# Two triangular inverses in step: interleaving the head pairs of an RWKV-7 scan on one Trainium2 core

## The chip, the cores and the metric

The kernel runs on one core of a Trainium2 chip. The metric is the device time of one execution in microseconds. Five engines matter: TensorE (matrix products, shown as PE, its weight loads as PEld), VectorE (DVE), ScalarE (ACT), GpSimd (POOL) and SyncE (SP), which issues most transfers.

## The reference

One inference step of a hybrid decoder layer over 576 tokens: a prompt of 512 and eight sequences of 8 sampled tokens. RWKV-7 time mixing and differential attention run as parallel branches on the same normalised input; their results are merged by gates, and a squared-ReLU MLP follows.

```python
xn = rmsnorm(x, lp['g_mix'], NORM_EPS)
P = xn @ lp['w_in']                                   # 1024 -> 5376 columns
o_a, S = rwkv7_branch(Pr, S0, lp)                     # 8 heads of 64
att = attend(q, k, v, lam)                            # 4 heads, two maps each
m = gate_a * (o_a @ lp['w_br_a']) + gate_b * (o_b @ lp['w_br_b'])
x = x + m @ lp['w_out']
x = x + jnp.square(jax.nn.relu(hn @ lp['w_up'])) @ lp['w_down']
```

What the change touches is the scan of the RWKV branch. As the reference has it, one token at a time:

```python
def step(S, inp):
    r_t, w_t, k_t, v_t, a_t, b_t = inp
    sa = jnp.einsum('bhij,bhj->bhi', S, a_t)
    S = S * w_t[:, :, None, :] + sa[..., None] * b_t[:, :, None, :] + v_t[..., None] * k_t[:, :, None, :]
    return S, jnp.einsum('bhij,bhj->bhi', S, r_t)
```

## The kernel before

**Chunks and pairs.** The kernel runs the scan in chunks of 64 tokens: eight of the prompt and one that holds the 64 sampled tokens. Within a chunk the recurrence becomes a unit triangular 64x64 system, whose inverse is computed once for each chunk and head; then a chain walks over the chunks. The eight heads are taken as four pairs, hp 0 to 3, two heads on the 128 partitions; pairs 0 and 1 form one group, 2 and 3 the other, and a group has one chain.

**Stages of a pair.** `rwkv(hp)` is a generator (L720 to L952). Its parts, which the text calls stages by letters, end at a `yield`:

- A: decay, normalised keys and the masked product matrices ABR (tiles pn, pw, pa, pk, pbn, pA; long on VectorE);
- B: transposed values and keys, and the sampled sequences' initial states (pV, pK, pI);
- C: the inverse (below);
- D: final states of the sampled sequences (pF);
- E: group norm, with a power on GpSimd and a multiplication of y by var on VectorE;
- F: output, with transposes pTy and the gate product pg.

**The inverse (L852 to L900).** X and its transpose Y hold the inverses of the diagonal blocks of size 1, 2, 4, 8, 16 and at the end 32. Four levels double the size. A level masks the matrix into DM (VectorE), makes W from DM and X by 32x32 products in the bank pW, copies W out (ScalarE), makes pZ from Y and W, adds it to X (VectorE), and transposes X into Y (VectorE). Each of these two visits of TensorE has 72 products of 32x32 by 32x32 (64 in the last two levels). Then Wc and pC, 32 products each, join 32 to 64, and TT takes the result. Every step needs the one before, so TensorE is given dense work between the visits.

**Dense work.** All large matrix products (`stream`, L154) are generators that issue one product at each step: 128x128 weights against 288 columns (296 for some of the projections). They run in split precision, three products for each block of weights; the weights come by SP's queue, ScalarE and VectorE split them into a high and a low half, and each half span of 24 products has one of two PSUM banks (pool psd). The list `waiting` holds such generators in order: the projections z of pairs 1 to 3 (144 products a pair), eight gates of branch B, five of branch A (48 each), later the output of branch B and three more gates. `take(n)` issues the next n products of that list.

**Order.** The framework orders each engine's instructions at build time by a model of durations: among those ready, the one first in program order goes. `issue_after` holds the instructions of its block back until the named one on the same engine has been issued. In the inverse `blocks` takes nine dense products so, behind each of the eight visits. Where the program stands at each moment is written by hand at the end (L1027 to L1055): `run(...)` advances the named pairs by a stage each, `take` stands between.

**Banks.** The inverses use the bank of `tbank`. `cbank(1)`, another pool's, is used by the attention before and by the output pY of the chain (L972) after.

Of the kernel before, what the change touches and what calls it, by code (L numbers as in the profile page):

```python
# [41 lines left out]
def tile_hybrid_step(ctx, tc, xT, xsT, ktab, vtab, s0T, ptab, w_in, vecs, w2a2, g2, lamv,  # L42
# [6 lines left out]
    def pool(name, bufs=1, stack=ctx, **kw):  # L49
        return stack.enter_context(tc.tile_pool(name=name, bufs=bufs, **kw))  # L50
# [4 lines left out]
    ring = {"job": 0}  # L55

    def act(out, in_, func=AF.Copy, **kw):
        ring["act"] = AE.activation(out=out, in_=in_, func=func, **kw)  # L58

    def tt(out, a, b, op, eng=None):  # L60
        ins = (eng or VE).tensor_tensor(out=out, in0=a, in1=b, op=op)  # L61
        if eng is None:
            ring["tt"] = ins
# [7 lines left out]
    def mm(out, lhsT, rhs, start=True, stop=True):  # L71
        ring["mm"] = PE.matmul(out=out, lhsT=lhsT, rhs=rhs, start=start, stop=stop)  # L72
        return ring["mm"]
# [17 lines left out]
    MUL, ADD, SUB, MAX = ALU.mult, ALU.add, ALU.subtract, ALU.max  # L91
# [12 lines left out]
    def tbank(name):  # L104
        return psc.tile([P, 512], F32, tag="t", name=name)

    def cbank(i, name):
        return (psy if i else psc).tile([P, 512], F32, tag=f"c{i}", name=name)
# [107 lines left out]
    def take(n):  # L216

        while waiting and n:
            if next(waiting[0], None) is None:
                waiting.pop(0)  # L220
            else:
                n -= 1
# [41 lines left out]
    gs = pool("gs", 2, stack=ph1)  # L264

    with tc.tile_pool(name="xin", bufs=2, reuse_waits="tile") as xin:
# [6 lines left out]
        for k in range(0, KT, 4):  # L273
            for j in range(3):
                with prio(FEED + 1000 + 10 * k + j):
                    name = f"raw_{'qkv'[j]}0_{k}"
# [142 lines left out]
    def shifted(i):  # L419
        z = zw.tile([P, 1 + NX], F32, tag="z", name=f"Z{i}")  # L420
        GE.memset(z[:, 0:1], 0.0)

        def f(ps, t0, n):
            tt(z[:, 1 + t0:1 + t0 + n], ps, R1[:, t0:t0 + n], MUL)
        yield from stream(w_in[i], KT, xh, xl, HALFX, f, f"z{i}")
        tz = zw.tile([P, 1 + NX], F32, tag="tz", name=f"tz{i}", bufs=1)
        act(tz, z, scale=v(V_MU + i))
        p = zp.tile([P, NT], F32, tag=f"P{i}" if i >= 12 else f"Pt{i // 4}", name=f"P{i}", bufs=1 if i >= 12 else 2)
        m1 = mu1[:, i:i + 1]
        stt(p[:, :NPR], z[:, 1:1 + NPR], m1, tz[:, 0:NPR], MUL, ADD)  # L430
        s3 = lambda a, o: a[:, o:o + NS].rearrange("p (b t) -> p b t", b=NB)
        stt(s3(p, NPR)[:, :, 1:], s3(z, 1 + NPR)[:, :, 1:], m1, s3(tz, 1 + NPR)[:, :, :7], MUL, ADD)
        stt(p[:, NPR::8], z[:, 1 + NPR:1 + NT:8], m1, tz[:, 1 + NT:], MUL, ADD)
        Pt[i] = p

    def zs(hp):
        return [shifted(i) for i in (hp, 4 + hp, 8 + hp)]

    def gate(g):

        gg = gs.tile([P, NT], F32, tag="gg", name=f"gg{g}")

        def ev(ps, t0, n):
            tt(gg[:, t0:t0 + n], ps, R1[:, t0:t0 + n], MUL)
            act(gg[:, t0:t0 + n], gg[:, t0:t0 + n], AF.Tanh, scale=0.5)
        yield from stream(w_in[26 + g], KT, xh, xl, HALF, ev, f"g{g}")
        nc.sync.dma_start(out=gt_d[g], in_=gg)
# [20 lines left out]
    def branch_b(d):  # L468

        if not ob:  # L470
            ob.extend(ob_halves())
        gg = rt.tile([P, NT], F32, tag="T", name=f"gb{d}", bufs=6)
        nc.sync.dma_start(out=gg, in_=gt_d[KT + d])

        def ev(ps, t0, n):
            stt(gg[:, t0:t0 + n], gg[:, t0:t0 + n], 1.0, ps, ADD, MUL)
        yield from stream(w_brb[d], HB, ob[0], ob[1], HALF, ev, f"brb_{d}")
        nc.sync.dma_start(out=gt_d[KT + d], in_=gg)
# [221 lines left out]
    def m3(ap_, n):  # L700
        q, w = ap_.shape
        return ap_.rearrange("p (o w) -> p o w", o=1).broadcast_to([q, n, w])
# [17 lines left out]
    def rwkv(hp):  # L720
        e = hp % 2
# [131 lines left out]
        for g in range(4):  # L853
            gs = slice(32 * g, 32 * g + 32)
            act(DT[gs], ABR[gs, :, 0, 32 * (g % 2):32 * (g % 2) + 32])
        Y = rt.tile([P, NCH, 32], F32, tag="Y", name=f"Y{hp}", bufs=2)
        X = rt.tile([P, NCH, 32], F32, tag="X", name=f"X{hp}", bufs=2)
# [1 line left out]
        tt(Y, Y, m3(c[:, C_I32:C_I32 + 32], NCH), ADD)  # L859
        VE.transpose(out=X, in_=Y)  # L860

        def blocks(ps, lhs, rhs, n):
            for ci in range(n):
                for g in range(4):
                    gs = slice(32 * g, 32 * g + 32)
                    last = mm(ps[gs, ci * 32:ci * 32 + 32], lhs[gs, ci], rhs[gs, ci])
            with tc.issue_after(last.ins):
                take(9)
            return ps[:, :n * 32].rearrange("p (c s) -> p c s", c=n)

        with tc.issue_after(ring["mm"].ins):
            take(1)
        for l in range(1, 5):

            n = NCH if l < 3 else 8
            DM = rt.tile([P, NCH, 32], F32, tag="DM", name=f"DM{hp}_{l}")
            tt(DM[:, :n], DT[:, :n], m3(c[:, C_LM + 32 * l:C_LM + 32 * l + 32], n), MUL)
            W = rt.tile([P, NCH, 32], F32, tag="W", name=f"W{hp}_{l}")
            act(W[:, :n], blocks(tbank(f"pW{hp}{l}"), DM, X, n))
            tt(X[:, :n], X[:, :n], blocks(tbank(f"pZ{hp}{l}"), Y, W, n), ADD)  # L880
            VE.transpose(out=Y[:, :n], in_=X[:, :n])
        TT = rb_.tile([P, NCH, 64], F32, tag="TT", name=f"TT{hp}")
        pW = tbank(f"pWc{hp}")
        W = rt.tile([P, NCH, 32], F32, tag="W", name=f"Wc{hp}")
        quads = [(slice(64 * par, 64 * par + 32), slice(64 * par + 32, 64 * par + 64)) for par in range(2)]
        for ci in range(8):
# [1 line left out]
                mm(pW[b1, ci * 32:ci * 32 + 32], ABR[b0, ci, 0, 32:64], X[b0, ci])  # L888
        for b0, b1 in quads:
            act(W[b1, :8], pW[b1, :256].rearrange("p (c s) -> p c s", c=8))  # L890
        pC = tbank(f"pC{hp}")
        for ci in range(8):
            for b0, b1 in quads:
                mm(pC[b0, ci * 32:ci * 32 + 32], W[b1, ci], Y[b1, ci])
        for b0, b1 in quads:
            act(TT[b0, :8, 32:64], pC[b0, :256].rearrange("p (c s) -> p c s", c=8))
            act(TT[b0, :, 0:32], Y[b0])
            act(TT[b1, :, 32:64], Y[b1])
            GE.memset(TT[b0, 8:, 32:64], 0.0)
            GE.memset(TT[b1, :, 0:32], 0.0)  # L900

        own[e] = ST, KBt, TT, ABR, pc
        yield
# [113 lines left out]


    gens = [rwkv(hp) for hp in range(4)]

    def run(*stages):
        for hp in stages:
            while Pt[8 + hp] is None:
                take(2)
            next(gens[hp], None)

    waiting += zs(1) + zs(2) + zs(3) + [gate(g) for g in range(KT, 2 * KT)]  # L1027
    ga = [gate(g) for g in range(KT)]
    waiting += ga[:5]
    run(0, 0)  # L1030
    take(221)
    run(0, 1, 1)
    take(106)
    run(1)
    chain(0)
    run(2, 0, 1, 2, 3)
    take(291)
    run(2, 0, 1, 3)
    take(38)
    run(3)  # L1040
    waiting += [x for d in range(KT) for x in [branch_b(d)] + ga[5:][d:d + 1]]
    run(0, 1)
    chain(1)
# [237 lines left out]
    for t0, n in LAST:  # L1281
        span, last = slice(t0, t0 + n), []
# [172 lines left out]
```

## Time and profile before

| | us |
|---|---|
| three timed runs | 1013.26, 1016.58, 1019.81 |
| median | 1016.58 |
| the profiled execution | 1013.8 |
| its span | 1012.0 |
| mean granted TensorE clock | 0.989 of full speed |

The span runs from the first to the last instruction that the profile shows; 1.8 us lie around it. "Busy" of TensorE is the time in which at least one product was in its pipeline, so that it isn't the same as TensorE at its peak. A row of the order in time has the start, the duration from the first start to the last end, the engine, the line (often a helper's, such as L72, the one of all products, or L58 and L61), the operation, output and inputs by the program's names, the shape, and the count. In brackets stands the idle time ahead of it on its engine, with what ended it. A row of a table by stretches has, after the stretch and its length, the busy time of PE, PEld, DVE, ACT and POOL (of one engine where a single engine or tile is asked for), each with its count, then the granted clock, the share of the transfer engines and GB/s. The stretch of the four inverses and two chains runs from about 227 to 492 us.

### The profile page before, as it was taken

How to read it: one execution, taken by the hardware profiler on the slowest of the kernel's cores; microseconds unless marked ns; L12 is line 12 of the kernel's file. 1: busy time of each engine (PE TensorE's matmuls, PEld its weight loads, DVE VectorE, ACT ScalarE, POOL GpSimd, SP SyncE). 2: the span in 40 equal slices, each digit the busy share in tenths (PEclk: the TensorE clock that was granted, in tenths of full speed). 3: DMA queues.
4: the chain of work that ended last, by engine and by line, in shares of the span. 5: the costliest groups of instructions: out<-in, count | busy, mean ns of one | idle time of the engine just before them, and what ended most of it. 6: DMA issues, size and time to landing. Idle time of an engine off the chain costs nothing. (4 is left out here: it accounts for less than half of the span.)

```text
span 1012.0 us, 24407 instructions
## 1 busy us (share of the span) xinstructions
PE 976.8 (97%) x10012; PEld 918.6 (91%) x10012; DVE 694.5 (69%) x1445; ACT 495.7 (49%) x1086; POOL 101.0 (10%) x179
## 2 busy tenths in 40 slices
PE   8999989999999998999989999999999999999996
PEld 8999978898888888878789999999999999999996
DVE  6698665864965788344579888966666666666744
ACT  6576554353544353453244666644444444444732
POOL 2511102301010431000210111000000000000001
PEclk9999999999999999999999999999999999999998
DMA  7412564121111135312367632222222222221402
GB/s 264 150 66 86 181 204 135 44 66 52 53 45 58 58 111 160 99 68 92 114 207 220 198 121 99 76 102 85 94 84 87 92 85 84 85 84 43 134 3 94
DMA packets 50834, 105.75 MB, mean 104 GB/s; under 512 B 6067, under 2 KB 8115, under 8 KB 50595
## 3 DMA queue, kind: packets, MB, share of 16 engines
q1 hardware_dynamic: 47442, 96.95, 29.9%
q0 software_dynamic: 1648, 5.35, 1.4%
q10 hardware_dynamic: 1632, 1.89, 0.5%
q8 instruction: 79, 1.29, 0.5%
q14 instruction: 33, 0.26, 0.1%
HBM read 89.38 MB, written 14.78 MB: 103 GB/s over the span
## 5 line engine op out<-in xcount | busy, mean ns | idle before, releaser
L72 PE MATMUL ps_dn<-q,hi_dn 128*128 128x288 f32 x768 | 154.8, 296 | 0.0
L72 PEld LDWEIGHTS ps_dn<-q,hi_dn 128*128 128x128 f32 x768 | 122.9, 188 | 1.4
L72 PE MATMUL ps_dn<-q,lo_dn 128*128 128x288 f32 x384 | 113.3, 295 | 0.0
L72 PE MATMUL ps_g<-xh,hi_g 128*128 128x288 f32 x256 | 80.2, 313 | 0.0
L72 PE MATMUL ps_g<-xh,lo_g 128*128 128x288 f32 x256 | 79.0, 308 | 0.0
L72 PE MATMUL ps_g<-xl,hi_g 128*128 128x288 f32 x256 | 78.9, 308 | 0.0
L72 PEld LDWEIGHTS ps_dn<-q,lo_dn 128*128 128x128 f32 x384 | 72.1, 188 | 0.0
L72 PE MATMUL ps_z<-xh,hi_z 128*128 128x296 f32 (+1 forms) x224 | 67.8, 303 | 1.3 <-DVE Z L61 0.7
L72 PE MATMUL ps_z<-xh,lo_z 128*128 128x288 f32 (+1 forms) x224 | 68.6, 306 | 0.0
L72 PE MATMUL ps_z<-xl,hi_z 128*128 128x288 f32 (+1 forms) x224 | 67.9, 303 | 0.0
L61 DVE TENSOR_TENSOR ya<-ya,ps_dn 128x288 f32<-128x288 f32 x96 | 43.3, 451 | 29.4 <-PE ps_dn L72 29.4
L58 ACT ACTIVATE hi_dn<-raw_dn 128x512 fp32r<-128x512 f32 x48 | 30.1, 628 | 56.1 <-PE ps_dn L72 56.1
L1191 PE MATMUL ua<-h_b,hi 128*128 128x288 f32 x256 | 53.3, 299 | 0.9 <-ACT p L58 0.9
L1191 PE MATMUL ux<-h_t,hi 128*128 128x288 f32 x256 | 52.3, 296 | 0.0
L58 ACT ACTIVATE c<-c 128x288 f32<-128x288 f32 x112 | 48.5, 439 | 6.5 <-DVE c L61 4.9
L72 PEld LDWEIGHTS ps_g<-xl,hi_g 128*128 128x128 f32 x256 | 48.7, 190 | 2.5 <-issue 0.8
L72 PEld LDWEIGHTS ps_g<-xh,hi_g 128*128 128x128 f32 x256 | 48.7, 190 | 2.5 <-issue 0.8
L72 PEld LDWEIGHTS ps_g<-xh,lo_g 128*128 128x128 f32 x256 | 48.6, 190 | 1.4
L58 ACT ACTIVATE hi<-a 128x1024 fp32r<-128x1024 f32 (+1 forms) x32 | 27.0, 845 | 43.0 <-PE ps_dn L72 34.8
L61 DVE TENSOR_TENSOR lo<-s,hi 128x1024 fp32r<-128x1024 f32 x32 | 39.2, 1224 | 10.5 <-ACT hi L58 10.4
L72 PE MATMUL ps_dn<-q,w 128*128 128x320 f32 (+1 forms) x336 | 46.3, 298 | 0.0
L72 PEld LDWEIGHTS ps_dn<-q,w 128*128 128x128 f32 x336 | 45.2, 190 | 0.1
(399 smaller groups left out, 2816.0 us busy)
## 6 DMA issues: line engine op xcount, KB each, us to landing
a<-in_w_up_dram SPq DMA_DIRECT2D x32, 512.0 KB, 3.3
raw_dn<-in_w_down_dram SPq DMA_DIRECT2D x64, 256.0 KB, 2.8
raw_g<-in_w_in_dram SPq DMA_DIRECT2D x32, 256.0 KB, 3.1
raw_z<-in_w_in_dram SPq DMA_DIRECT2D x28, 256.0 KB, 2.9
gt_d<-gg SPq DMA_DIRECT2D x16, 288.0 KB, 2.4
g<-gt_d SPq DMA_DIRECT2D x16, 288.0 KB, 3.4
kp<-in_ktab_dram SPq DMA_DIRECT2D x16, 256.0 KB, 4.7
vp<-in_vtab_dram SPq DMA_DIRECT2D x16, 256.0 KB, 4.2
```

The costliest lines, as they stand in the source:

```text
L58: ring["act"] = AE.activation(out=out, in_=in_, func=func, **kw)
L61: ins = (eng or VE).tensor_tensor(out=out, in0=a, in1=b, op=op)
L72: ring["mm"] = PE.matmul(out=out, lhsT=lhsT, rhs=rhs, start=start, stop=stop)
L1191: ring["mm"] = PE.matmul(out=ps[:, :288], lhsT=l[:, k], rhs=hb[blk][:, h, k], start=start and i == 0, stop=i == 11, skip_group_check=skip)
```

## The change

The inverse yields behind each visit instead of taking dense products itself. `invert(0, 1)` and `invert(2, 3)` step two pairs in turn, and take six dense products behind each double visit. The second pair of a group has the chain's output bank instead of the shared one. So that both are ready, pair 1's stages A and B come ahead of pair 0's inverse, and stage E of pairs 0 and 1 and stage B of pair 3 come ahead of the joint inverse of 2 and 3. The free takes change with it: 106 becomes 150, 291 becomes 340; those of an inverse were 73 for one pair and are 61 for two. What isn't taken there stays in the list for later.

```diff
-        def blocks(ps, lhs, rhs, n):
+        def blocks(name, lhs, rhs, n):
+            ps = cbank(1, name) if e else tbank(name)
             for ci in range(n):
                 for g in range(4):
                     gs = slice(32 * g, 32 * g + 32)
-                    last = mm(ps[gs, ci * 32:ci * 32 + 32], lhs[gs, ci], rhs[gs, ci])
-            with tc.issue_after(last.ins):
-                take(9)
+                    mm(ps[gs, ci * 32:ci * 32 + 32], lhs[gs, ci], rhs[gs, ci])
             return ps[:, :n * 32].rearrange("p (c s) -> p c s", c=n)
 
-        with tc.issue_after(ring["mm"].ins):
-            take(1)
         for l in range(1, 5):
...
-            act(W[:, :n], blocks(tbank(f"pW{hp}{l}"), DM, X, n))
-            tt(X[:, :n], X[:, :n], blocks(tbank(f"pZ{hp}{l}"), Y, W, n), ADD)
+            act(W[:, :n], blocks(f"pW{hp}{l}", DM, X, n))
+            yield True
+            tt(X[:, :n], X[:, :n], blocks(f"pZ{hp}{l}", Y, W, n), ADD)
             VE.transpose(out=Y[:, :n], in_=X[:, :n])
+            yield True
...
-        pW = tbank(f"pWc{hp}")
+        pW = cbank(1, f"pWc{hp}") if e else tbank(f"pWc{hp}")
...
+        yield True
-        pC = tbank(f"pC{hp}")
+        pC = cbank(1, f"pC{hp}") if e else tbank(f"pC{hp}")
...
+    def invert(*hps):
+
+        with tc.issue_after(ring["mm"].ins):
+            take(1)
+        more = True
+        while more:
+            for hp in hps:
+                more = next(gens[hp], None)
+            with tc.issue_after(ring["mm"].ins):
+                take(6)
+
     waiting += zs(1) + zs(2) + zs(3) + [gate(g) for g in range(KT, 2 * KT)]
     ga = [gate(g) for g in range(KT)]
     waiting += ga[:5]
     run(0, 0)
     take(221)
-    run(0, 1, 1)
-    take(106)
-    run(1)
+    run(1, 1)
+    take(150)
+    invert(0, 1)
     chain(0)
     run(2, 0, 1, 2, 3)
-    take(291)
-    run(2, 0, 1, 3)
+    take(340)
+    run(0, 1, 3)
     take(38)
-    run(3)
+    invert(2, 3)
```

## The prediction

> **What bounds the kernel now.** I read the page from the top, then the share of each engine in the stretch that the change touches (220 to 500 us), then the order of TensorE's instructions there, then VectorE's at the one place where TensorE stands still.
>
> ```profile
> span 1012.0 us, 24407 instructions
> ...
> PE 976.8 (97%) x10012; PEld 918.6 (91%) x10012; DVE 694.5 (69%) x1445; ACT 495.7 (49%) x1086; POOL 101.0 (10%) x179
> ```
>
> TensorE is the bound: 35 us of the span are left idle, spread over the kernel. A gain must come from idle time or from time in which TensorE counts as busy and does little. Both can be seen in the inverses. First one visit of pair 0 (its 72 small products), in order of time; columns are start, duration, instruction, count.
>
> ```profile
> 227.07 0.29 PE L72 MATMUL ps_z<-xl,hi_z 128*128 128x288 f32 x1
> 227.29 0.82 PE L72 MATMUL pW<-X,DM 32*32 32x32 f32 x72
> 228.04 0.40 PE L72 MATMUL ps_z<-xh,lo_z 128*128 128x288 f32 x1
> 228.27 0.29 PE L72 MATMUL ps_z<-xh,hi_z 128*128 128x288 f32 x1
> 228.40 0.29 PE L72 MATMUL ps_z<-xl,hi_z 128*128 128x288 f32 x1
> ...
> 229.20 0.29 PE L72 MATMUL ps_z<-xl,hi_z 128*128 128x288 f32 x1
> 229.43 0.82 PE L72 MATMUL pZ<-W,Y 32*32 32x32 f32 x72
> ```
>
> From 228.27 to 229.20 lie seven dense products: 0.133 us each. The median small product lasts 0.19 us:
>
> ```profile
> L72 PE MATMUL pW<-X,DM x1088: 185/192/257, 227.3 to 440.0; 32*32 32x32 f32 x182
> ```
>
> so the last of the 72 starts 0.82 - 0.19 = 0.63 us after the first: 8.9 ns apart. A visit's period is 229.43 - 227.29 = 2.14 us. Nine dense products take 1.19, 72 small ones 0.64; **0.31 us are left over, the price of going from dense to small and back**. It sits at the edges: dense to small takes 0.22 instead of 0.13, and the first dense product behind the block holds the next off for 0.23.
>
> Second, pair 2's third visit, on TensorE and on VectorE.
>
> ```profile
> 397.05 0.29 PE L72 MATMUL ps_g<-xh,lo_g 128*128 128x288 f32 x1
> 400.03 1.18 PE L72 MATMUL pW<-X,DM 32*32 32x32 f32 x72 [2.69 <-DVE X L61]
> 401.15 0.61 PE L72 MATMUL ps_g<-xh,hi_g 128*128 128x288 f32 x1
> ...
> 403.56 0.82 PE L72 MATMUL pZ<-W,Y 32*32 32x32 f32 x72
> ```
>
> ```profile
> 396.05 0.74 DVE L61 TENSOR_TENSOR obh<-ob,obh 128x576 fp32r<-128x576 f32 x1
> 398.49 0.76 DVE L61 TENSOR_TENSOR y<-y,var 128x576 f32<-128x576 f32 x1 [1.69 <-POOL var L238]
> 399.16 0.45 DVE L61 TENSOR_TENSOR Y<-DT,cst_sb 128x288 f32<-128x288 f32 x1
> 399.53 0.45 DVE L61 TENSOR_TENSOR X<-X,pZ 128x288 f32<-128x288 f32 x1
> ```
>
> The group norm of pairs 0 and 1 (y times var, stage E of the program) stands in VectorE's queue ahead of pair 2's X and waits 1.69 us for GpSimd's power; the products allowed at this point are used up, and TensorE idles. Without the wait the block would have started at 397.05 + 0.22 = 397.27: 2.76 us lost. Then the granted clock (the column behind the busy times) falls:
>
> ```profile
> 398.00:400.00 2.00, 0.00 (x0) 0.00 (x0) 1.51 (x4) 0.00 (x0) 1.29 (x5) 1.00 0.37 133
> 400.00:402.00 2.00, 1.97 (x75) 1.91 (x76) 2.00 (x6) 0.85 (x2) 0.00 (x0) 0.51 0.19 67
> 402.00:404.00 2.00, 2.00 (x57) 1.77 (x59) 1.70 (x4) 0.00 (x0) 0.00 (x0) 0.64 0.69 213
> ```
>
> and that visit takes 403.56 - 400.03 = 3.53 us for 2.14: 1.39 us more. **The stall costs 4.15 us.** [...]
>
> **The change, part by part.**
>
> *Half the switches.* Before, each of 4 pairs makes 10 visits (8 of blocks, then Wc and pC), each with a switch to small and back: 40. After, the two pairs' blocks follow each other: 20 double visits. Nothing else changes in the small work, and the dense products taken out of the visits are done elsewhere at 0.133. So 20 x 0.31 = 6.2 us. The price of small to small across two pairs isn't in the trace: from below nothing, as between the small products within a block; from above the same 0.31, and the saving is nil. I take nothing: every small product has its own weights already, so the pair's edge is like any other. [...]
>
> *Stage E leaves pair 2's inverse.* It is now put after `take(340)`, ahead of the joint inverse of 2 and 3. GpSimd's power and VectorE's wait for it remain, but in a stretch where dense products are free to go: minus 4.15. What it costs if that cover fails: up to the same, in another place. Pair 1's inverse has a small wait of the same kind:
>
> ```profile
> 292.17 0.75 PE L72 MATMUL pW<-X,DM 32*32 32x32 f32 x64 [0.55 <-DVE X L61]
> ```
>
> I count it as gone: minus 0.55.
>
> *Slack in a double visit.* The added wait: the six products stand behind the second pair's block, and the dense streams are in order (two banks), so all dense work queues behind that block when its X or W is late. Own block to own next block is the partner's 0.64 + 6 x 0.133 + 0.31 = 1.75 us, against 1.19 + 0.31 = 1.5 before.
>
> ```profile
> 228.15 0.41 ACT L58 ACTIVATE W<-pW 128x288 f32<-128x288 f32 x1
> ```
>
> ```profile
> 230.29 0.46 DVE L61 TENSOR_TENSOR X<-X,pZ 128x288 f32<-128x288 f32 x1 [0.74 <-PE pZ L72]
> 230.78 0.48 DVE L881 STREAM_TRANSPOSE Y<-X 128x288 f32<-128x288 f32 x1
> ```
>
> W needs 0.45 us. For X: the block that began at 229.43 ends at 230.25, X is ready at 230.75, 0.50 later. The second pair's X stands behind the first's X and Y (0.46 + 0.48): 0.94 + 0.50, less the 0.64 by which its block ends later, 0.80 of 1.75. So about 1 us is spare; it hides one foreign VectorE instruction of the size above (0.45 to 0.76), not two. No cost.
>
> *Pair 1's preparation comes ahead.* It must be done before the joint inverse can go on. Before, from its first product to its X:
>
> ```profile
> 245.52 1.28 PE L72 MATMUL pn<-cst_sb,sq 128*128 128x2 f32 x10
> ```
>
> ```profile
> 281.35 0.47 DVE L860 STREAM_TRANSPOSE X<-Y 128x288 f32<-128x288 f32 x1
> ```
>
> 36.3 us, mostly VectorE's. The dense products beside it (two names, counts in brackets) were
>
> ```profile
> 245.50:283.00 37.50, 17.60 (x115) 1.00 0.15 43
> ```
>
> ```profile
> 245.50:283.00 37.50, 2.52 (x16) 1.00 0.15 43
> ```
>
> 131, 17.4 us of the 37.5. After, it begins where pair 0's inverse began (227.3), with 24 products of its own and `take(150)`: 174, 43 more or 5.7 us; what falls out is pair 0's Wc and pC, 0.7 us each. So TensorE has 37.5 + 5.7 - 1.4 = some 42 us of work, of which some 4 are pair 2's first products, pulled ahead as filler. VectorE gets the 43 products' splits and evacuations too: per 48 products two splits (0.69), two evacuations (0.47) and three shifts (1.08),
>
> ```profile
> 237.83 0.47 DVE L61 TENSOR_TENSOR Z<-ps_z,R 128x296 f32<-128x296 f32 x1 [1.29 <-PE ps_z L72]
> 238.36 0.69 DVE L61 TENSOR_TENSOR lo_z<-raw_z,hi_z 128x512 fp32r<-128x512 f32 x1
> ...
> 239.30 1.08 DVE L66 SCALAR_TENSOR_TENSOR P<-Z,mu,tz 128x512 f32<-128x512 f32 x3
> ```
>
> 3.4 us, or 3.0 for 43. Preparation 39.3 against 38 to 42: this is the tight place. Bounds: nothing, and 4 us if the filler isn't pulled. I take 1.
>
> *The second joint inverse.* By its start the program has asked for 24 + 221 + 24 + 150 + 61 + 40 + 340 + 8 + 38 + 1 = 907 products, 54 more than before pair 2's inverse (24 + 221 + 73 + 24 + 106 + 73 + 40 + 291 + 1 = 853): 7.2 us, and pair 3's stage B, some 3 us; 10 switches fewer save 3.1. So TensorE gets there at about 393 + 7 = 400. Chain 0 begins 41 products (5.4 us) and 3.1 us earlier, so pair 3 does too; its X, at 401.9 now, comes at some 394:
>
> ```profile
> 401.93 0.47 DVE L860 STREAM_TRANSPOSE X<-Y 128x288 f32<-128x288 f32 x1
> ```
>
> Six us spare. No cost.
>
> *The rest.* The odd pair's bank is the chain's output bank, so the first step's output products, done as filler before the inverse today, come after it: at most 0.4 us a chain, filled by dense work; nothing. DMA: weights keep their order on SP; pair 1's state load moves ahead with its stage, the stores of the last gates and the branch B loads move some 77 products (10 us) later. No TensorE wait in this stretch names a DMA. The 77 products come after chain 1, ahead of the merge, where TensorE waits today:
>
> ```profile
> 528.83 0.53 PE L72 MATMUL ps_bra<-oab,hi_bra 128*128 128x288 f32 x2 [0.16 <-DVE gb L66]
> 529.80 0.53 PE L72 MATMUL ps_bra<-oab,hi_bra 128*128 128x288 f32 x2 [0.31 <-ACT oab L58]
> 530.84 0.40 PE L72 MATMUL ps_bra<-oab,hi_bra 128*128 128x288 f32 x1 [0.50 <-DVE oab L61]
> ```
>
> They may hide this 1 us; I count nothing.
>
> **Sum.** 6.2 + 4.15 + 0.55 - 1 = 9.9 us off the profiled execution's 1013.8 (span 1012.0 and 1.8 around it): **1004 us**. The three runs' median is 1016.6, 0.3% above that execution, their lowest 1013.3; I stay with the sum.
>
> **Rivals.**
> - *The joint inverse starves at its start.* Pair 1's preparation is late, pair 0 waits with it, and no other dense work may pass. For: the two sums above nearly meet, and VectorE is nearly full there. Against: TensorE found filler of 4 us in the same place before. Price: the upper bound 4 in place of 1, plus a clock dip of 1.4: 1008.4. [...]
> - *The 0.31 us belongs to each block, not to the switch* (first weights, new bank), or other work is ordered between the two blocks so that the change doesn't pair them. For: nothing in the trace shows two pairs' blocks touching. Against: dense products with new weights and banks follow each other at 0.133. Then 3.7 us remain: 1010.
> - *Slower.* VectorE's queue becomes the bound: fillers with a wait for GpSimd (pair 2's preparation in the first joint inverse, stage E in the second) are ordered ahead of an X, as at 398.49, with only 6 products (0.8 us) behind instead of 9 (1.2). Each costs 4.15; from three on the sum turns; with four, 1004 + 16.6 = 1020.5. For: one in four inverses had it. Against: the queue's order puts the inverse's instructions first when ready.
>
> **How the numbers follow.** Forecast 52% (1000 to 1007), of it some 5% with the merge's wait gone as well (down to 999); starving 22%; price per block 18%; slower 8%. A measurement of this kernel tells about 1%. The forecast lies on that bound (1.0% under the profiled execution, 1.2% under the median), so nearly all the chance of "faster by over 1%" is a bit less than the forecast's: 0.50. Starving, price per block and part of the slower case stay within 1%: 0.46. Slower by over 1%: 0.04. The range 998 to 1012 takes in the forecast, its upside, starving and price per block; of these ends and the slower case some 15% are left out.
>
> **What would show it.** In the profile after: blocks of 144 (later 128) small products with six dense ones behind, a double period near 1.28 + 0.8 + 0.31 = 2.4 us; no wait of pW for X of over 1 us, granted clock at 1.00 from 390 to 450; TensorE's idle time some 2 us less (the two stalls, less the 1 us added), its busy time some 7 to 8 less (switches and dip count as busy). Wrong if the double period is 2.7 (price per block), if the first odd block waits for X or DM (starving), or if a row of y, var or nr waits for GpSimd ahead of an X.

## The result, and the profile after

| | before | after |
|---|---|---|
| median of six runs each, us | 1015.08 (1012.34 to 1019.81) | 1040.22 (1034.03 to 1046.44) |
| ratio, 95% interval | | 1.0242 [1.0214, 1.0271] |
| profiled execution, us | 1013.8 | 1046.4 |

The change makes the kernel 2.4% slower, 25.1 us by the medians; 1004 was forecast. The profiled execution of after is the slowest of its six, so the accounts below explain 32.7 us of one execution and not the 25.1 of the median. The page of after, its span, its engines and the granted clock in 40 slices:

```profile
span 1044.7 us, 24407 instructions
...
PE 992.2 (95%) x10012; PEld 935.0 (90%) x10012; DVE 696.7 (67%) x1445; ACT 497.2 (48%) x1086; POOL 98.8 (9%) x179
...
PEclk9999999999959989869999999999999999999999
```

The same 10012 products, 32.7 us more: 52.5 us idle for 35.2 (+17.3) and 15.4 us more busy time. A slice is 26.1 us; the clock falls to 0.5 in the 12th (287 to 313) and to 0.8 and 0.6 in the 17th and 18th (418 to 470): at the two joint inverses. (The 0.8 in the 15th, 366 to 392, stands behind two waits for data in the pairs' preparation, of 2.12 and 1.53 us.) Who ends TensorE's waits, before and then after (total us, times, longest):

```profile
PE pZ L72 <- issue: 1.0, 3, 0.4
PE pW L72 <- issue: 0.5, 1, 0.5
```

```profile
PE pZ L72 <- issue: 9.8, 8, 2.3
PE pW L72 <- issue: 6.7, 5, 1.8
PE ps_g L72 <- issue: 2.5, 2, 1.9
```

In the joint inverses no data is late: every wait of TensorE that the profile lists there is one for issue, and the waits of pW for X (3.2 us before) are gone. "Issue" is time in which the engine waited for nothing that the profile shows. There are 17.5 us more of it, as much as the idle time grew; the other waits changed too (pA waits 2.4 us for ST where it waited 0.2), but they come to 33.7 us in all before and to 33.5 after. The small products, those of 32x32, of the first joint inverse in order of time (dense rows left out):

```profile
264.80 1.45 PE L72 MATMUL pW<-X,DM 32*32 32x32 f32 x144
...
267.18 0.89 PE L72 MATMUL pZ<-W,Y 32*32 32x32 f32 x81
...
269.26 0.74 PE L72 MATMUL pZ<-W,Y 32*32 32x32 f32 x63 [1.19 <-issue]
...
270.95 0.70 PE L72 MATMUL pW<-X,DM 32*32 32x32 f32 x59
...
272.99 0.95 PE L72 MATMUL pW<-X,DM 32*32 32x32 f32 x85 [1.34 <-issue]
...
274.86 0.52 PE L72 MATMUL pZ<-W,Y 32*32 32x32 f32 x37
...
276.72 1.15 PE L72 MATMUL pZ<-W,Y 32*32 32x32 f32 x107 [1.34 <-issue]
```

The first double visit goes as forecast: 267.18 - 264.80 = 2.38 us. Then the stalls cut through the middle of a block, at an equal count: 63 small, 6 dense and 59 small between the first two are 128; 85, 6 and 37 are 128. The page counts as many weight loads as products, 10012 of each, so the 128 products between two stalls are 256 instructions: **TensorE stops every 256 instructions here**, and goes on 3.73 us after the last time (269.26, 272.99, 276.72). Between one stall and the next lies such a block throughout the two joint inverses, with 15 stalls (once it is two blocks; the count of products is right within one), and a block takes 3.7 to 4.3 us. The transfers of the stretch from 262 to 300 us show what comes in that rhythm (40 slices of 0.95 us, and a queue's packets, MB, share):

```profile
GB/s 69 207 0 0 17 9 60 194 39 0 0 0 17 0 0 179 97 17 0 0 0 17 0 0 0 17 0 0 17 0 0 0 17 0 0 0 0 17 0 0
...
q8 instruction: 9, 0.15, 1.7%
```

The instruction queue brings nine transfers of 0.15 / 9 MB = 16 KB, in the right half the lone "17" three to five slices apart (17 GB/s times 0.95 us is 16 KB): 64 bytes for each of 256 instructions. Each of the lone transfers stands 1.1 to 1.5 us behind the moment at which TensorE goes on with a block, and 2.6 to 2.8 us ahead of the next such moment, where there is a stall. **In the joint inverses TensorE's instructions arrived at about 128 products in 3.7 us, 34 a microsecond** (30 at the longest interval, 4.28 us). The queue uses 1.7% of the transfer engines, and all transfers together 8 and 12% in the two joint inverses (below), so these engines aren't what is short; whether a block is asked for late or takes long was not shown.

A dense product takes 0.133 us, 7.5 a microsecond, far under that supply. A single visit with nine dense products is 81 in 2.14 us, 38 a microsecond: just over it. In the kernel before, three of the four inverses have a wait for issue, the first of each 12 to 16 us behind the inverse's start; by my estimate a stock of half a block to one carries them so far (4 products a microsecond over 12 to 16 us, and 11 over 12.6 in single6, below). A double visit with six is 150 in 2.4 us, 62 a microsecond. By stretches, the two joint inverses with what follows each (length, busy time, clock), and the same rows for two of the four inverses of before:

```profile
264.80:305.10 40.30, 31.17 (x1279) 0.76 0.08 24
305.10:315.00 9.90, 9.90 (x65) 0.61 0.15 56
425.99:467.60 41.61, 31.77 (x1274) 0.70 0.12 34
467.60:480.00 12.40, 12.40 (x104) 0.77 0.17 55
```

```profile
227.30:248.30 21.00, 20.53 (x698) 1.00 0.17 54
...
393.00:416.20 23.20, 20.50 (x688) 0.93 0.37 112
```

By the forecast's terms a joint inverse is 4 x 2.39 + 4 x 2.25 + 2 x 2.1 = 22.8 us (eight double visits, four of them with 128 small products, then Wc and pC; their 2.1 is the 3.46 us from one to the other in joint16, below, less ten dense products). At full clock, by the mean granted clock of the stretch, its busy time would be about that, an estimate: 31.17 x 0.76 = 23.7 and 31.77 x 0.70 = 22.2. The rest is 9.1 and 9.8 us of idle time, and the lower clock measured beside the stalls (0.76 and 0.70, for 1.00 and 0.93 in the two inverses of before). Over plan: 17.5 and 18.8 us. Behind them the clock stays low: 9.90 x 0.39 = 3.9 and 12.40 x 0.23 = 2.9. Together 43.1; less the 9.9 forecast, 33.2 slower, for 32.7 measured in the span. That close a sum is partly chance, since not all of the 9.9 came, as orderonly shows below, and other waits in the pairs' preparation grew.

### The profile page after: what moved, and what is told of

Read it like the earlier page. It is cut to its first block, busy times and chain, and to the rows that moved or that the text cites. A ratio compares the mean times of both kernels' runs of the same rounds, so it can differ in the third digit from the quotient of the medians.

```text
span 1044.7 us, 24407 instructions
## 1 busy us (share of the span) xinstructions
PE 992.2 (95%) x10012; PEld 935.0 (90%) x10012; DVE 696.7 (67%) x1445; ACT 497.2 (48%) x1086; POOL 98.8 (9%) x179
## 4 chain that ended last, share of the span: by engine, by line
PE 78%; DVE 7%; issue 5%; ACT 4%; DMA 4%; POOL 1%; SPq 0%; DVEq 0%; ACTq 0%; POOLq 0%
PE ps_dn L72 19%; PE ps_g L72 9%; PE ps_z L72 6%; PE ua L1202 5%; PE ux L1202 5%; PE uc L1202 3%; PE ps_bra L72 2%; PE ub L1202 2%; PE ps_k L72 2%; PE ud L1202 2%; PE pch L72 2%; PE ps_brb L72 2%; PE ps_q L72 2%; DMA kp<-in_ktab_dram 2%; PE pZ L72 1%
## 5 line engine op out<-in xcount | busy, mean ns | idle before, releaser
L72 PE MATMUL ps_g<-xh,hi_g 128*128 128x288 f32 x256 | 84.4, 330 | 1.9 <-issue 1.9
L72 PE MATMUL ps_g<-xh,lo_g 128*128 128x288 f32 x256 | 83.9, 328 | 0.6 <-issue 0.6
L72 PE MATMUL ps_g<-xl,hi_g 128*128 128x288 f32 x256 | 82.5, 322 | 0.0
L72 PEld LDWEIGHTS ps_g<-xl,hi_g 128*128 128x128 f32 x256 | 52.5, 205 | 4.1 <-issue 2.8
L72 PEld LDWEIGHTS ps_g<-xh,lo_g 128*128 128x128 f32 x256 | 52.1, 203 | 2.6 <-issue 0.8
L72 PEld LDWEIGHTS ps_g<-xh,hi_g 128*128 128x128 f32 x256 | 51.9, 203 | 2.2
```

## The experiments

Theory: supply. What counts is how many TensorE instructions a microsecond the inverse asks for. Rivals: the order of the stages (late preparation), the interleaving itself (banks, pair edges), VectorE's queue. The free `take` counts differ in some kernels so that the list is used up as far as before; those lines are left out of the edits shown, and so is the bookkeeping of the loop.

**single6: the kernel before with denser visits**, six dense products for nine.

```diff
             with tc.issue_after(last.ins):
-                take(9)
+                take(6)
```

> The kernel before, one pair at a time, with six dense products behind a visit in place of nine; the 24 that fall out of each inverse are added to the free takes ahead. Theory of supply (TensorE's instructions arrive at no more than 256 in about 3.73 us, a product with its weight load being two): a visit of 72 + 6 products takes 78 / 128 x 3.73 = 2.27 us, more than the 2.14 that it took with nine; rows of 'issue' inside the blocks of small products, 128 products apart; time about 1019. Rival (the loss comes from two pairs waiting for each other, or from the stage order): the visit shortens to 0.64 + 0.80 + 0.31 = 1.75 us, no waits of 'issue' beyond those of before, time 1013 to 1015.

1024.77 us, 1.0107 [1.0077, 1.0137]. Order of time, then the waits:

```profile
226.72 0.82 PE L72 MATMUL pW<-X,DM 32*32 32x32 f32 x72
...
228.47 0.82 PE L72 MATMUL pZ<-W,Y 32*32 32x32 f32 x72
```

```profile
PE pW L72 <- issue: 2.3, 3, 1.6
PE pZ L72 <- issue: 1.9, 2, 1.5
```

The period is 1.75 us: 78 products, 45 a microsecond, 10 or 11 over the supply. A stock of one block of 128 would last 12 us at that; the first stall (0.89 us) ends at 239.34, 12.6 us after the start. Fewer products between the visits cost time, though the work is the same: waits for issue rise from 1.5 us to 5.9 over all tiles, as supply has it. The time is above the forecast of 1019; a wait of pA for ST of 2.7 us came in as well (below), so that not all of the 1.1% need be supply's.

**twice: the kernel before, each small product of the eight block visits issued twice**, which leaves the result as it is.

```diff
-                    last = mm(ps[gs, ci * 32:ci * 32 + 32], lhs[gs, ci], rhs[gs, ci])
+                    for _ in range(2):
+                        last = mm(ps[gs, ci * 32:ci * 32 + 32], lhs[gs, ci], rhs[gs, ci])
```

> The kernel before, one pair at a time, with each small product of the eight block visits issued twice (the same result written again). Theory of supply: a visit of 144 + 9 products takes 153 / 128 x 3.73 = 4.46 us, an inverse (1152 + 73) / 128 x 3.73 = 36 us in place of 21, all four 58 us more: about 1073, with the clock falling in the stalls perhaps more. Rival (TensorE's own work sets the visit): 0.64 us more a visit, 20 us for all 32: about 1035, and no waits of 'issue' of 1 us and over.

1070.5 us (two executions), 1.0562 [1.0522, 1.0602].

```profile
228.50 0.50 PE L72 MATMUL pZ<-W,Y 32*32 32x32 f32 x34 [1.00 <-issue]
...
230.31 1.05 PE L72 MATMUL pW<-X,DM 32*32 32x32 f32 x85
...
232.23 0.79 PE L72 MATMUL pW<-X,DM 32*32 32x32 f32 x59 [0.86 <-issue]
```

No pairs in step here, no other order, and the stalls are the same: 34 + 9 + 85 = 128 products between two, 3.73 us apart. The instruction queue counts along, on the page of before and on that of twice:

```profile
q8 instruction: 79, 1.29, 0.5%
```

```profile
q8 instruction: 96, 1.57, 0.6%
```

The 2176 products more (12188 for 10012), two instructions each, are 17 x 256, and the queue brings 17 blocks more: it is TensorE's.

**joint16: after with 16 dense products behind each double visit.**

```diff
             with tc.issue_after(ring["mm"].ins):
-                take(6)
+                take(16)
```

> The changed kernel with 16 dense products behind each double visit in place of six, the free takes cut to 160, 150 and 280 so that the list is used up as far as before. Theory of supply: a joint inverse takes (1216 + 161) / 128 x 3.73 = 40 us, hardly more than with six (37), though it holds 100 products (13 us) more; waits of 'issue' shrink from 1.3 to some 0.7 us each, still 128 products apart; time about 1012 to 1018. Rival (the second pair's block waits for its X or W): such waits, named DVE or ACT, vanish with the longer cover and the double visit takes TensorE's work, 1.28 + 2.13 + 0.31 = 3.7 us: 1003.

1013.1 us, 0.9991 [0.9974, 1.0008]: the whole loss comes back.

```profile
271.12 1.48 PE L72 MATMUL pZ<-W,Y 32*32 32x32 f32 x144
...
274.91 1.31 PE L72 MATMUL pW<-X,DM 32*32 32x32 f32 x128
...
278.50 1.35 PE L72 MATMUL pZ<-W,Y 32*32 32x32 f32 x128
...
282.10 1.31 PE L72 MATMUL pW<-X,DM 32*32 32x32 f32 x128
```

Where nothing stalls, the period of 128 small products is 3.59 and 3.60. The prediction's terms give 1.14 + 16 x 0.133 + 0.31 = 3.58: one switch. With a price at each block it would be 3.89. The waits for issue are not gone, though: 9.5 us over all tiles, for 19.0 in after and 1.5 before. 144 products in 3.59 us are 40 a microsecond; from 267.04 on, five such visits pass before the next stall, which ends at 285.81. Between that one and the next, which ends at 289.36, TensorE took 128 products (127 in the rows) in 3.55 us, 36 a microsecond, so 34 is no fixed rate.

**orderonly and alt9: after's order of the stages and its banks.** In the first the inverses go one after the other, nine dense products behind each visit; in the second the pairs are in step as in after, with nine behind each single block.

```diff
-            with tc.issue_after(ring["mm"].ins):
-                take(6)
+            if i < 8:
+                with tc.issue_after(ring["mm"].ins):
+                    take(9)
...
-    invert(0, 1)
+    invert(0)
+    invert(1)
```

```diff
             for hp in hps:
-                more = next(gens[hp], None)
-            with tc.issue_after(ring["mm"].ins):
-                take(6)
+                next(gens[hp], None)
+                if i < 8:
+                    with tc.issue_after(ring["mm"].ins):
+                        take(9)
```

> The changed kernel's stage order and banks, but the inverses one after the other, nine dense products behind each of the eight block visits; free takes 190, 150 and 280. Theory of supply: density is that of before, so visits take 2.1 us again with at most short waits of 'issue', and what the stage order brings shows alone: the stall on the norm is gone, 1009 to 1012. Rival (the stage order, pair 1's preparation ahead of pair 0's inverse, costs the time): 1030 or more, with TensorE's idle time ahead of the first inverses.

> The changed kernel with the two pairs still in step, but nine dense products behind each single block instead of six behind two; free takes 190, 150 and 280. Density is that of the kernel before. Theory of supply: 2.1 us for each single visit, waits of 'issue' as before, about 1013. Rival (two pairs in step, with their shared engines and second bank, cost the time): 1025 and more, with waits for W, X or the bank.

1013.46 us, 0.9998 [0.998, 1.0017], and 1014.98, 1.0012 [0.9991, 1.0033]. Neither the order nor the step brings the loss: **it is the density**. But orderonly was to gain 4 us by stage E's move. The wait of pW for X (3.2 us) is gone from it; yet its idle time is 39.7 us for 35.2 (its profiled execution, 1017.04, is the slowest of its ten). Issue has 4.7 us over all tiles for 1.5, and these stand in the stages A and B of pairs 2 and 3:

```profile
367.87 1.11 PE L72 MATMUL pI<-ST,s 64*64 64x16 f32 x32 [1.26 <-DMA s<-in_s0T_dram]
...
373.36 0.66 PE L76 MATMUL pk<-cst_sb,nb 128*128 128x128 f32 x4 [0.87 <-POOL nb L741]
...
385.80 1.24 PE L72 MATMUL pbn<-rkp,cst_sb 128*128 128x288 f32 x4 [1.12 <-DVE rkp L66]
...
401.41 0.33 PE L76 MATMUL pV<-cst_sb,P 128*128 128x128 f32 x1 [0.75 <-ACT SVU L58]
```

All waits for data in these preparations come to 5.4 us, for 2.5 in the kernel before, and to 4.4 in alt9. But joint16, with the same order, has 2.8, so the order alone doesn't make them.

**e_first: the kernel before with stage E called first**, ahead of pair 2's inverse.

```diff
-    run(2, 0, 1, 3)
+    run(0, 1, 2, 3)
```

> The kernel before with one edit: stage E of pairs 0 and 1 stands ahead of pair 2's inverse in the program, not behind it. If the stall of 2.7 us on the norm and its clock dip are there in every execution and go with the edit, as the prediction had it: 4 us less, 1010. Rival: VectorE's order hardly changes, since the norm was already placed as early as its inputs allowed, or the wait moves to another instruction: 1013 to 1015, the wait for GpSimd's power still ahead of an X.

1015.47 us, 1.0001 [0.9976, 1.0025]: no gain, as the rival had it. The rows on VectorE and on TensorE:

```profile
397.08 0.76 DVE L61 TENSOR_TENSOR y<-y,var 128x576 f32<-128x576 f32 x1 [1.69 <-POOL var L238]
```

```profile
399.29 1.18 PE L72 MATMUL pW<-X,DM 32*32 32x32 f32 x72 [2.65 <-DVE X L61]
```

The wait stays: moving the call alone did not take the norm from ahead of X. That the order by modelled durations puts it there was not shown.

**single11: e_first with eleven behind each visit.** `take(9)` becomes `take(11)`.

> The kernel before with stage E ahead of pair 2's inverse, and eleven dense products behind a visit in place of nine, the free takes cut by 16 an inverse. Theory of supply: a visit of 83 products takes TensorE 2.40 us, and its instructions 83 / 128 x 3.73 = 2.42: the supply just suffices, the waits of 'issue' inside the inverses (2 us before) all but vanish; 1 to 2 us below the run with nine. Rival (waits of 'issue' come at random, whatever the density): unchanged.

1017.5 us, 1.0022 [1.0002, 1.0042]: a miss. The waits for issue fell (pZ 0.8, pW 0.2), as supply has it, and a wait of pA for ST of 2.3 us came.

**joint20, joint12b, joint16b: other densities in after.** 20, 12 and 16 dense products behind the block visits, six behind Wc and pC.

```diff
-                take(6)
+                take(20 if i < 8 else 6)
```

> The changed kernel with 20 dense products behind each of the eight double block visits and six behind the two of Wc and pC; free takes 140, 145 and 281, so that the list is used up as far as before. Theory of supply: a double visit of 128 + 20 products needs 148 / 128 x 3.73 = 4.31 us for its instructions and 1.14 + 2.66 + 0.31 = 4.11 of TensorE: nearly equal, so waits of 'issue' fall to 0.2 us each and half of the switches' saving stays: 1007 to 1011, at or a little below the kernel before. Rival (a double visit loses time of its own, by its second pair's waits): no better than with 16, 1013 and over, with waits named DVE or ACT.

> The changed kernel with 12 dense products behind each of the eight double block visits and six behind the two of Wc and pC; free takes 195, 160 and 339, list used up as far as before. Theory of supply: a double visit of 128 + 12 products needs 140 / 128 x 3.73 = 4.08 us for its instructions and 1.14 + 1.60 + 0.31 = 3.05 of TensorE: 1 us of stall a visit, 16 us in all, less the 7 saved: 1018 to 1025. Rival (any cover longer than six mends it): as with 16, 1011 to 1014.

> As the run with 12, with 16 behind the block visits and free takes 172, 155 and 303: more free cover ahead of the joint inverses than the runs with 16 and 20 had. Theory of supply: 0.6 us of stall a visit, some 8 in all, against 7 saved: about the kernel before, 1010 to 1014. If what eats the switches' saving in the run with 20 was the lack of cover in the pairs' preparation (waits of pA and pbn for VectorE), those waits shrink below 1 us here and the time is 1010; if not, 1015.

1014.97 us, 1.0013 [0.9989, 1.0037]; 1028.75, 1.0134 [1.0105, 1.0164]; 1021.74, 1.0081 [1.005, 1.0112]. From 6 to 12 to 16 to 20 the time falls, 1040, 1029, 1022, 1015, as supply has it, and so do the waits for issue: 19.0, 12.0, 8.2, 4.9. But all three are slower than expected, by 4 us for joint20 and joint12b and 8 for joint16b. joint20's time is the one that its rival had, and waits for VectorE are there, but in the pairs' preparation; the joint inverses have 0.2 us of them. And joint16b is 8 us over joint16, from which it differs behind Wc and pC and in the free takes alone; all three have a wait of pA for ST of 2.6 us. (joint16b against joint16: 5.3 us more idle time, 4.2 of it in pA and pbn, and 4.3 more busy time, with a granted clock of 0.91 for 1.00 between 300 and 340 us.) In joint20:

```profile
340.82 3.92 DVE L66 SCALAR_TENSOR_TENSOR ST<-sq,u 64x576 f32<-64x576 f32 x1
341.08 3.04 POOL L61 TENSOR_TENSOR vm<-SVU,cst_sb 128x512 f32<-128x512 f32 x3
...
344.66 0.75 DVE L61 TENSOR_TENSOR ST<-P,pe 64x576 f32<-64x576 f32 x1
...
347.00 1.13 PE L72 MATMUL pA<-ST,KB 128*128 128x128 f32 x8 [2.60 <-DVE ST L61]
```

An instruction of 0.75 us took 3.92 here beside three vm of GpSimd in a row. The kernel before has a small case of it, and so has joint16:

```profile
344.12 3.70 POOL L61 TENSOR_TENSOR vm<-SVU,cst_sb 128x512 f32<-128x512 f32 x3
344.31 1.60 DVE L61 TENSOR_TENSOR ST<-P,pe 64x576 f32<-64x576 f32 x1
```

Here ST took 1.60 us, and the three vm 3.70 for 3.04.

**joint20v and beforev: vm on VectorE**, in joint20 and in the kernel before.

```diff
             tt(vm, m3(SVU[:, 8, par], NB),
-               c[:, C_MB:C_MB + NB].rearrange("p (b o) -> p b o", o=1).broadcast_to([P, NB, 64]), MUL, GE)
+               c[:, C_MB:C_MB + NB].rearrange("p (b o) -> p b o", o=1).broadcast_to([P, NB, 64]), MUL)
```

> The kernel of twenty dense products behind each double visit (1014.97 us), with one edit: the four masks of the sampled values (tile vm), two for each of two pairs in each group, move from GpSimd to VectorE. It isolates a collision read from the traces: a VectorE product into ST, 0.75 us at most in the kernel before, took 3.9 us where it ran beside GpSimd's vm of 3.04 us, and TensorE waited 2.60 us for ST and then ran at a lower clock. Theory of the collision: no instruction into ST over 1 us, no wait of pA for ST over 1 us, and the time falls by 3 to 5 us, to about 1010 to 1012. Rival (the ST was late for another reason, or another wait takes its place): the wait of pA stays over 2 us, or it goes and the time stays at 1014 to 1016.

> The kernel before with the same edit alone: vm on VectorE in place of GpSimd. Both theories: the kernel before has no wait of pA for ST, so the time stays within 1013 to 1017; VectorE gets some 2 to 3 us more work, GpSimd loses about 24 us (8 times 3.04). If it is slower by more, VectorE's queue is nearer to the bound than the idle time of TensorE in the kernel before says.

(A vm takes 1.04 us; the 3.04 in the expectations are three of them, so GpSimd loses 8.3 us, not 24. And the longest ST in the kernel before takes 1.60 us, not 0.75. The granted clock of joint20 was 1.00 from 344 to 360 us, behind the wait of 2.60, and 0.96 over 340 to 380.) joint20v: 1012.57 us, 0.9977 [0.9957, 0.9996]. No instruction into ST is over 0.76 us, and pA waits no more: the collision is shown. What it is worth is not: the median is 2.4 us lower, less than was expected, and the two intervals overlap. Another wait has come, in joint20v

```profile
PE pTy L76 <- DVE y L61: 2.6, 1, 2.6
```

and the same in beforev, which at 1018.85, 1.0045 [1.0022, 1.0068], is a little beyond its expectation. The wait there, and the clock behind it:

```profile
514.89 1.33 PE L76 MATMUL pTy<-cst_sb,y 128*128 128x128 f32 x5 [2.58 <-DVE y L61]
```

```profile
515.00:520.00 5.00, 4.54 (x15) 0.50 0.03 8
520.00:525.00 5.00, 5.00 (x34) 0.84 0.51 170
```

Pair 3's group norm comes 2 us later there (its y is multiplied at 514.08 for 512.10), with no dense work left to cover it. joint20v is the only one of the kernels whose interval lies below 1, by 0.2%, with its end at 0.9996; among so many that is no clear gain.

## Why the prediction was wrong

- **Half the switches** (minus 6.2). Price and pairing were right: 3.59 us for 3.58 in joint16, whose busy time is 6.3 us under that of before (970.5 for 976.8); that this is so close to 6.2 is partly luck, since the clock's dips, which differ in the two, are in it. The step that failed is its sentence "Nothing else changes in the small work". The small products stay the same, but they come closer together, at 62 a microsecond where the instructions arrived at 34. The trace of before had a hint, which I didn't quote: 1.5 us of waits of pZ and pW for issue, all of them in the inverses, where 38 a microsecond are asked for, and each 12 to 16 us behind an inverse's start. I read TensorE's idle time by its largest wait and not by that name.
- **Slack in a double visit** (no cost). For VectorE and ScalarE right: no X is late in after. The double period of 2.4 us held for the first visit of each joint inverse (2.38 in both).
- **Stage E leaves pair 2's inverse** (minus 4.15, and 0.55 for pair 1's wait). Both waits are gone, and in orderonly the busy time is 1.3 us lower, near the 1.39 that the prediction gave to the clock's dip (that it is this dip was not shown). What came in their place there is in the next two points, and 3.2 us more of waits for issue.
- **Pair 1's preparation comes ahead** (plus 1). About right: in orderonly it waits 0.58 us for rkp, 0.44 for KBt and 0.24 for SVU, 1.26 in all, where pair 1's preparation waited 0.38 and 0.32 for the first two before.
- **The second joint inverse** (at about 400, six us spare, no cost). It started at 425.99; 21.4 of the 26 us are the first's loss and its dip. But the cost was not nothing in orderonly: the preparation of pairs 2 and 3 waits 2.9 us more than before, and that and the waits for issue are more than stage E's move had saved. I asked whether X would be in time, not what TensorE waits for on the way there; the DMA among the rows above is a state load, for which I counted nothing. Which of the moved stages makes which wait was not taken apart, and why joint16 hasn't them stays open.
- **The rivals.** Starving didn't show, as pW and DM were in time; the price per block is refuted; the rival on the slower side had VectorE as its mechanism and appears in no wait. The kernel slowed by more than any of them had, through a resource that no part of the sum had. All three looked at data; none at instructions.

What stays open: why a block of instructions took 3.7 us and more with the transfer engines 8 and 12% busy, and how much stock TensorE holds (half a block to one, by the first stalls; an estimate).

## What to carry to other kernels

Count TensorE's instructions for each microsecond, not its busy time alone. Many small products with weights of their own ran into the supply here, at about 34 a microsecond, and large products between them were not only filler but time in which instructions arrived: the waits for issue were 19.0, 12.0, 8.2 and 4.9 us with 6, 12, 16 and 20 of them (after, joint12b, joint16b, joint20). Before packing such work closer, look for waits for "issue" in the stretch, and for stalls at an equal count of instructions; in this kernel waits of 0.2 to 0.5 us were the only sign that the stretch was at the limit already.

## What the runs showed of the hardware

The clock fell without a gap as long as the 2.69 us of before: in the first joint inverse no gap was over 1.88 us, and yet the mean granted clock was 0.76 in it and 0.61 for the 9.9 us behind, where TensorE was busy throughout. That the stalls are the cause was not shown: the run twice, with 28.4 us of waits for issue, has a mean granted clock of 0.987, after 0.965 and before 0.989.

VectorE was held up beside GpSimd: in joint20 an instruction of VectorE of 0.75 us took 3.92, until GpSimd's three products (341.08 to 344.12) were done; it was 3.87 in single11, beside the same tile. In the kernel before the one took 1.60, and GpSimd's three 3.70 for 3.04. The delay went when vm left GpSimd, with no instruction into ST over 0.76 us in joint20v; what in the chip makes it no run shows.
